# The four 64-column matmuls of each state-space group pair: alternating between PSUM's halves, and held together

## The chip, the cores and the metric

The kernel runs on one core of a Trainium2 chip. A core has a matrix engine (TensorE), engines for elementwise work (VectorE, ScalarE, GpSimd), queues that issue transfers (SyncE among them), an on-chip memory of 128 partitions (SBUF) and a smaller one for matmul results (PSUM, also 128 partitions, in eight banks). The metric is the time on the device in microseconds (us), taken as the median over runs. Lower is better.

## The reference

One layer of a hybrid encoder, in float32, for 2048 tokens of width 1024. A normalised input goes through one wide projection, which feeds three branches: a "forgetting" attention of 12 heads, a state-space layer with a gated unit, and a cross attention into 256 memory tokens. The gated branches are projected back, merged, projected once more and added to the input. The part that matters here is the state-space layer, 48 groups of 16 channels, each with 64 complex states:

```python
    x_re = jnp.einsum('gph,blgh->blgp', bb_re, uf)
    x_im = jnp.einsum('gph,blgh->blgp', bb_im, uf)
    ...
    _, _, h_re, h_im = lax.associative_scan(combine, (a_re, a_im, x_re, x_im), axis=1)
    y = (jnp.einsum('ghp,blgp->blgh', c_re.astype(f32), h_re)
         - jnp.einsum('ghp,blgp->blgh', c_im.astype(f32), h_im))
    y = y + d_skip.astype(f32).reshape(S5_GROUPS, S5_GROUP) * uf
```

The state runs over the tokens with a complex decay; the output is a linear function of the state plus a direct term.

## The kernel before

The large matrix products are made from float32 operands that are split into a high and a low part; `mm3` (lines 144 to 149) issues three matmuls for each product: high by high (line 147), the stationary operand's high by the moving one's low part (148), and the other way round (149). One projection chunk is an output tile of 128 channels by 512 tokens, 24 such matmuls into one PSUM bank (`proj_chunk`, tags `psA` and `psF`).

The state-space branch works in the shadow of these projections. `gen_s5` goes through 24 pairs of groups; `s5_pair` (from line 534) treats one pair, in chunks of 8 tokens:

- VectorE builds the matrix that says what a chunk adds to the state (`m1r`, `m1i`); TensorE transposes both (lines 550, 551), ScalarE copies them to SBUF (`m1t`).
- VectorE builds `z` and `bb`, from the decay's powers and the input and output matrices. Two matmuls of 16 output columns (line 572, tile `psB`) make the kernel by which a chunk's inputs act on its own outputs. ScalarE copies it (574), and nine transfers bring it through device memory into a banded matrix `m3`.
- Four matmuls of 64 output columns (line 585, tile `psC`) make what each chunk adds to the state: for each of the two groups, the real and the imaginary part. Their stationary operand is a slice of `m1t`, their moving one the pair's inputs `u` (256 columns). Group 0 writes PSUM partitions 0 to 63, group 1 partitions 64 to 127; real and imaginary part stand beside each other, so all four write one bank.
- VectorE builds a table of phases (lines 588 to 596), reads the four results (598 to 602), runs two real scans (605, 606) and turns the states back (`hs`).
- Four matmuls of 128 columns (625, 626) make the outputs from `m3`, `u`, `z` and `hs`; ScalarE copies them out, a transfer stores them.

```python
        pv = self.psC()
        for g in range(2):
            for ri in range(2):
                nc.tensor.matmul(pv[64 * g:64 * g + 64, ri * 256:(ri + 1) * 256],
                                 m1t[:, ri * 128 + 64 * g:ri * 128 + 64 * g + 64], u[:, g, :], start=True, stop=True)
```

Each step ends with a `yield`. `proj` alternates: for each projection chunk the side work may take some 1.7 steps (`RATE[0]`). This sets the program order, which is the order of priority. The order in which an engine gets its instructions is set by a planner: it simulates the kernel while it is built, and at each moment gives an engine the ready instruction that stands earliest in the program. An engine then works its queue off in that order. `issue_after(x)` tells the planner that what a block issues on the engine of `x` may be queued only behind `x`; it doesn't wait for the result of `x`. The kernel already uses it near its end (line 1038), to tie projection work to the attention.

Of the kernel before, what the change touches and what calls it, by code (L numbers as in the profile page):

```python
# [12 lines left out]
D = 1024  # L13
# [3 lines left out]
KD = 8  # L17
# [17 lines left out]
KS = 3  # L35
# [14 lines left out]
class Layer:  # L50
# [83 lines left out]
    def load_w(self, src, shape, pool=None, bufs=2):  # L134
        """One [128, 1024] slab of weights, split into two float32r parts."""
        raw = self.wp.tile([128, 4 * NV], F32, tag="wraw", name="wraw", bufs=2)
        k, m = shape
        n = k * m
        self.nc.sync.dma_start(out=raw[:, :n], in_=src)
        hi, lo = ((pool or self.wp).tile([128, n if bufs == 1 else 1024], F32R, tag=t, name=t, bufs=bufs) for t in ("whi", "wlo"))  # L140
        self.split(hi[:, :n], lo[:, :n], raw[:, :n])
        return (hi[:, :n].rearrange("p (k m) -> p k m", k=k), lo[:, :n].rearrange("p (k m) -> p k m", k=k))

    def mm3(self, out, a, b, first, last):
        """a = (hi, lo) stationary, b = (hi, lo) moving."""
        nc = self.nc
        nc.tensor.matmul(out, a[0], b[0], start=first, stop=False)  # L147
        nc.tensor.matmul(out, a[0], b[1], start=False, stop=False)  # L148
        nc.tensor.matmul(out, a[1], b[0], start=False, stop=last)  # L149

    def rsqrt(self, p, out, ssq, n):
        """out = 1 / sqrt(ssq / D + eps): table square root, then a Newton step."""
        nc = self.nc
        v = p.tile([128, n], F32, tag="nv", name="nv", bufs=2)
        t = p.tile([128, n], F32, tag="nt", name="nt", bufs=2)
        nc.vector.tensor_scalar(out=v, in0=ssq, scalar1=1.0 / D, scalar2=EPS, op0=ALU.mult, op1=ALU.add)
        nc.scalar.activation(t, v, AF.Sqrt)
        nc.vector.reciprocal(out, t)
        nc.vector.tensor_mul(t, out, out)
        nc.vector.tensor_mul(t, t, v)  # L160
        nc.vector.tensor_scalar(out=t, in0=t, scalar1=-0.5, scalar2=1.5, op0=ALU.mult, op1=ALU.add)
        nc.vector.tensor_mul(out, out, t)

    def norm_T(self, src, nt, g, hi, lo, p, xb, split=False):
        """RMSNorm of nt tiles of 128 tokens, then transposed and split: hi, lo [128, KD, nt*128]."""
        nc = self.nc
# [23 lines left out]

# [1 line left out]
    def open_h(self):  # L192
# [63 lines left out]
    def proj_v(self, g, p):  # L256
        """Values of four heads; the forget gates ride with the first four."""
        nc, s = self.nc, self.s
# [29 lines left out]
    def forget(self, p):  # L288
        """-F, the running sum of -log sigmoid(z)."""
        nc, z = self.nc, self.fz  # L290
        e = p.tile([H, L], F32, name="fe")
        nc.vector.scalar_tensor_tensor(out=e, in0=z, scalar=-1.0, in1=z, op0=ALU.mult, op1=ALU.max)
        nc.scalar.activation(e, e, AF.Exp, scale=-1.0)
        nc.scalar.activation(e, e, AF.Ln, bias=1.0)
        nc.vector.scalar_tensor_tensor(out=z, in0=z, scalar=0.0, in1=e, op0=ALU.min, op1=ALU.subtract)
        one = p.tile([H, 1], F32, name="fo")
        nc.vector.memset(one, 1.0)
        nc.vector.tensor_tensor_scan(e, one.to_broadcast([H, L]), z, 0.0, ALU.mult, ALU.subtract)
        nc.sync.dma_start(out=self.s["nf"], in_=e)
# [106 lines left out]

# [1 line left out]
    def s5_exp(self, p, out, x):  # L408
        """exp(x): range reduction by ln 2, polynomial, exact power of two."""
        v = self.nc.vector  # L410
# [14 lines left out]
    def s5_reduce(self, t, n):  # L425
        """t - 2 pi round(t / 2 pi), in place."""
        v = self.nc.vector
        v.tensor_scalar(out=n, in0=t, scalar1=0.15915494309189535, scalar2=12582912.0, op0=ALU.mult, op1=ALU.add)
        v.tensor_scalar(out=n, in0=n, scalar1=-12582912.0, scalar2=None, op0=ALU.add)
        for c in (6.28125, 2029.0 / 1048576.0, 3.0199159819e-7):  # L430
            v.scalar_tensor_tensor(out=t, in0=n, scalar=-c, in1=t, op0=ALU.mult, op1=ALU.add)

    def s5_sincos(self, p, sn, cs, t, n):
        """sin and cos of t in [-pi, pi] (t is overwritten) by the quarter angle and two doublings."""
        v = self.nc.vector
# [16 lines left out]
    def cmul(self, outr, outi, ar, ai, br, bi, t):  # L452
        """(outr, outi) = (ar, ai) (br, bi); t is scratch; the outputs are none of the inputs."""
        v = self.nc.vector
        v.tensor_mul(outr, ar, br)
        v.tensor_mul(t, ai, bi)
        v.tensor_sub(outr, outr, t)
        v.tensor_mul(outi, ar, bi)
        v.tensor_mul(t, ai, br)
        v.tensor_add(outi, outi, t)  # L460

    def s5_prep(self, q, p):
        """Discretised parameters in the layout [(group parity, state), group pair]; q keeps, p is scratch."""
        nc, v, i = self.nc, self.nc.vector, self.i
# [69 lines left out]
    def s5_pair(self, q, a):  # L534
        """Groups 2a and 2a+1. Chunks of 8 steps: what a chunk adds to the state (M1), the state at each chunk's
        end (a real scan of the states turned back by the phase they have run through), and the outputs from the
        state before the chunk (M2) and from the chunk's own inputs (M3)."""
        nc, v, s = self.nc, self.nc.vector, self.s
# [32 lines left out]
        for g in range(2):  # L571
            nc.tensor.matmul(ps[0:16, g * 128:(g + 1) * 128], bb[:, g, :], z[:, g, 0:128], start=True, stop=True)
        kd = q.tile([16, 2, 128], F32, tag="kd", name="kd", bufs=1)
# [8 lines left out]
        pv = self.psC()  # L582
        for g in range(2):
            for ri in range(2):
                nc.tensor.matmul(pv[64 * g:64 * g + 64, ri * 256:(ri + 1) * 256],  # L585
                                 m1t[:, ri * 128 + 64 * g:ri * 128 + 64 * g + 64], u[:, g, :], start=True, stop=True)
        er, ei, vr, vi, x, hr = t("er", 256), t("ei", 256), t("vr", 256), t("vi", 256), t("xx", 256), t("hr", 256)
# [53 lines left out]

# [1 line left out]
    def mem_scores(self, p, hd, j, b, P):  # L643
# [56 lines left out]

# [1 line left out]
    def open_fox(self):  # L702
# [3 lines left out]
    def fox_keys(self, h, c):  # L706
        """Half a head's keys (high over low parts), values (high beside low) and -F."""
        nc, s, p = self.nc, self.s, self.fp
# [21 lines left out]
    def fox_scores(self, p, hd, q, G, P):  # L730
        """Softmax rows of two blocks of 128 queries, the later one first: the mask goes into -F for good, as no
        later block of queries is left to read those keys unmasked."""
        nc = self.nc
# [31 lines left out]
    def fox_pv(self, p, h, hd, G, P):  # L765
        """Columns of the moving operand and of the sums: high parts of the two query blocks, then low parts."""
        nc, s = self.nc, self.s
# [41 lines left out]
    def gen_fox(self):  # L809
        """Heads one after the other, groups of queries from the last to the first; a head's last KS groups, the  # L810
        short ones, alternate with the next head's first ones."""
        p, self.close_f = self.pool("fox", side="right")
# [32 lines left out]

# [1 line left out]
    def gen_glu(self):  # L847
# [39 lines left out]
    def split(self, hi, lo, x, sc=1.0):  # L887
        """sc * x as hi + lo, each exact in float32r."""
        self.nc.gpsimd.tensor_scalar(out=hi, in0=x, scalar1=sc, scalar2=1.0, op0=ALU.mult, op1=ALU.mult)  # L889
# [7 lines left out]
    def ytile(self):  # L897
        """Slots of 4 KB, twelve in the first pool and ten in the second, in the order in which they come free."""
        i, self.ny = self.ny, self.ny + 1
# [20 lines left out]
    def gen_merge0(self):  # L920
        """The last chunk, under the last heads; its share of the attention as soon as the last head is past it."""
        nc, c = self.nc, NC - 1
# [129 lines left out]

# The channels of the state-space branch are kept, 128 at a time, in the order (channel of a group, group).
def host_arrays(x, mem, g_norm, g_mem_norm, g_final, w_in, b_forget, b_merge, w_mem_kv,
# [68 lines left out]
```

## Time and profile before

| | |
|---|---|
| time, median of 3 runs | 3076.02 us (3070.25 to 3080.53) |
| span of the profiled execution (its only time on the page) | 3072.7 us |
| TensorE matmuls, busy | 2995.7 us (97%) |
| VectorE, busy | 1884.8 us (61%) |
| GpSimd, busy | 1004.8 us (33%) |
| ScalarE, busy | 927.8 us (30%) |
| first and last start of the matmuls of line 585 | 405.3 and 927.1 us |
| granted TensorE clock, mean | 0.987 |

The profile is taken from one execution. "Busy" is the union of the times in which an engine has an instruction in flight; matmuls are pipelined, so several records can overlap, and the time from one start to the next says more than a duration. A float32 matmul of line 585 or 572 leaves two records. "L585" is line 585 of the kernel; `psC<-u,m1t` reads: writes `psC`, from `u` and `m1t`; "128*64" is the stationary operand (128 rows, 64 columns), "128x256" the moving one.

### The profile page before, as it was taken

The numbers are of one execution on the slowest core, as the hardware profiler recorded it, in microseconds if no ns is written. First come the engines' busy times: TensorE is split into PE (matmuls) and PEld (weight loads), VectorE is DVE, ScalarE is ACT, GpSimd is POOL, SyncE is SP. The second block draws the span as 40 slices with busy tenths as digits, with TensorE's granted clock in tenths as the row PEclk, the third lists the DMA queues.
The fourth block names the chain that finished last, engine by engine and source line by source line (L and its number), as shares of the span: only waits on it lengthen the run. The fifth ranks groups of instructions, "written<-read, shape, count | busy, mean of one in ns | idle before, by whom it ended". The sixth has DMA issues, their size and how long they took to land.

```text
span 3072.7 us, 43527 instructions
## 1 busy us (share of the span) xinstructions
PE 2995.7 (97%) x14656; PEld 2438.1 (79%) x14656; DVE 1884.8 (61%) x4982; ACT 927.8 (30%) x1881; POOL 1004.8 (33%) x1328
## 2 busy tenths in 40 slices
PE   9999999999999999999999999999999998999999
PEld 7889977777777778888878888888887786777787
DVE  5333489888886673322217777777777886555544
ACT  5102111111112231222216666666666550000011
POOL 0010000000001332121205665655555766555500
PEclk9999999999999999999999999999999998999999
DMA  5343323323344655344352443544434536665531
GB/s 167 107 136 96 105 84 116 115 84 111 114 132 150 175 164 173 108 127 136 115 165 82 124 121 103 134 121 121 118 111 130 145 108 195 185 182 172 159 108 69
DMA packets 283118, 396.81 MB, mean 129 GB/s; under 512 B 83060, under 2 KB 147828, under 8 KB 282884
## 3 DMA queue, kind: packets, MB, share of 16 engines
q1 hardware_dynamic: 275696, 381.39, 41.8%
q10 hardware_dynamic: 7200, 12.66, 1.2%
q8 instruction: 116, 1.90, 0.3%
q14 instruction: 106, 0.87, 0.1%
HBM read 265.51 MB, written 128.42 MB: 128 GB/s over the span
## 4 chain that ended last, share of the span: by engine, by line
PE 80%; DMA 6%; DVE 5%; issue 4%; POOL 3%; ACT 1%; SPq 0%; DVEq 0%; POOLq 0%; ACTq 0%
PE psF L147 10%; PE psF L148 10%; PE psF L149 10%; PE psA L147 8%; PE psA L148 8%; PE psA L149 8%; PE psC L798 5%; PE psB L782 5%; PE psA L750 3%; PE psA L751 3%; PE psC L147 1%; PE psC L148 1%; PE psC L149 1%; PE psC L585 1%; PE psB L149 1%
## 5 line engine op out<-in xcount | busy, mean ns | idle before, releaser
L147 PE MATMUL psF<-hh,whi 128*128 128x512 f32 (+1 forms) x1160 | 470.2, 405 | 5.3 <-DVE elo L228 2.5
L889 POOL TENSOR_SCALAR whi<-wraw 128x1024 fp32r<-128x1024 f32 (+2 forms) x216 | 204.8, 949 | 795.2 <-PE psA L148 362.0
L149 PE MATMUL psF<-hh,wlo 128*128 128x512 f32 (+1 forms) x1160 | 460.5, 397 | 0.5 <-DVE wlo L891 0.5
L148 PE MATMUL psF<-hl,whi 128*128 128x512 f32 (+1 forms) x1160 | 460.7, 397 | 0.0
L891 DVE TENSOR_TENSOR wlo<-wraw,whi 128x1024 fp32r<-128x1024 f32 (+2 forms) x216 | 260.5, 1207 | 213.4 <-POOL whi L889 189.2
L147 PE MATMUL psA<-hh,whi 128*128 128x512 f32 (+1 forms) x816 | 322.5, 397 | 1.4 <-ACT hh L187 0.8
L148 PE MATMUL psA<-hl,whi 128*128 128x512 f32 (+1 forms) x816 | 322.9, 396 | 0.0
L149 PE MATMUL psA<-hh,wlo 128*128 128x512 f32 (+1 forms) x816 | 321.7, 395 | 0.8 <-DVE wlo L891 0.8
L786 DVE TENSOR_TENSOR Pt<-psB,Pt 128x512 fp32r<-128x512 f32 x336 | 226.2, 685 | 76.3 <-ACT Pt L785 73.9
L798 PE MATMUL psC<-Pt,v 128*128 128x512 f32 x864 | 266.7, 398 | 4.1 <-DVE Pt L786 3.5
L147 PEld LDWEIGHTS psF<-hh,whi 128*128 128x128 f32 x1160 | 219.6, 189 | 52.7 <-DVE elo L228 3.3
L149 PEld LDWEIGHTS psF<-hh,wlo 128*128 128x128 f32 x1160 | 219.5, 189 | 52.0 <-DVE wlo L891 0.9
L148 PEld LDWEIGHTS psF<-hl,whi 128*128 128x128 f32 x1160 | 219.8, 189 | 45.8 <-issue 0.4
L752 DVE CUSTOM_DVE_ANT_0 P<-psA,nf 128x512 f32<-128x512 f32 (+1 forms) x336 | 201.2, 627 | 48.1 <-PE psA L751 28.2
L785 ACT CAST Pt<-psB 128x512 fp32r<-128x512 f32 x336 | 191.9, 586 | 107.4 <-PE psB L782 60.4
L761 POOL TENSOR_SCALAR P<-P,rd 128x768 f32<-128x768 f32 (+1 forms) x240 | 193.2, 821 | 59.6 <-DVE rd L758 36.6
L750 PE MATMUL psA<-kk,qh 128*128 128x512 f32 (+1 forms) x480 | 184.1, 389 | 4.5 <-DVE mx L752 2.6
L147 PEld LDWEIGHTS psA<-hh,whi 128*128 128x128 f32 x816 | 154.1, 189 | 36.9 <-issue 1.6
L149 PEld LDWEIGHTS psA<-hh,wlo 128*128 128x128 f32 x816 | 154.5, 189 | 36.1 <-DVE wlo L891 1.2
L148 PEld LDWEIGHTS psA<-hl,whi 128*128 128x128 f32 x816 | 154.3, 189 | 33.9 <-issue 0.4
L798 PEld LDWEIGHTS psC<-Pt,v 128*128 128x128 f32 x864 | 154.2, 190 | 31.2 <-DVE Pt L786 6.8
L782 PE MATMUL psB<-ident,P 128*128 128x128 f32 x1200 | 177.4, 274 | 0.3 <-POOL P L761 0.2
(343 smaller groups left out, 6228.3 us busy)
## 6 DMA issues: line engine op xcount, KB each, us to landing
wraw<-in_w_in SPq DMA_DIRECT2D x90, 512.0 KB, 4.3
s_gl<-ehi SPq DMA_DIRECT2D x96, 256.0 KB, 2.5
g<-s_gl SPq DMA_DIRECT2D x96, 256.0 KB, 4.6
wraw<-in_w_proj SPq DMA_DIRECT2D x64, 320.0 KB, 2.9
s_vs<-ev_v SPq DMA_DIRECT2D x48, 256.0 KB, 2.7
nf<-s_nf SPq DMA_DIRECT2D x24, 512.0 KB, 6.4
v<-s_vs SPq DMA_DIRECT2D x24, 512.0 KB, 6.4
qh<-s_qh SPq DMA_DIRECT2D x96, 128.0 KB, 3.7
```

Source lines behind the costliest of these rows:

```text
L147: nc.tensor.matmul(out, a[0], b[0], start=first, stop=False)
L148: nc.tensor.matmul(out, a[0], b[1], start=False, stop=False)
L149: nc.tensor.matmul(out, a[1], b[0], start=False, stop=last)
L750: nc.tensor.matmul(ps[:, :wm], q[0][:, qs], kk[:, c0:c0 + wm], start=True, stop=False)
L752: nc.vector.tensor_tensor_reduce(out=pr[:, c * 512:c * 512 + w], in0=ps[:, :w], in1=nf[:, c0:c0 + w], scale=1.0, scalar=-3.0e38, op0=ALU.a ...
L761: nc.gpsimd.tensor_scalar(out=c, in0=c, scalar1=rd, scalar2=0.5, op0=ALU.mult, op1=ALU.mult)
L782: nc.tensor.transpose(ps[:, o:o + 128], P[b][:, kt * 128:(kt + 1) * 128], self.ident)
L785: nc.scalar.copy(hi, psv)
L786: nc.vector.tensor_sub(lo, psv, fl32(hi))
L798: self.pe = nc.tensor.matmul(o, v, m, start=(kt == 0), stop=(kt == 2 * G + 1))
L889: self.nc.gpsimd.tensor_scalar(out=hi, in0=x, scalar1=sc, scalar2=1.0, op0=ALU.mult, op1=ALU.mult)
L891: self.nc.vector.tensor_sub(lo, x, fl32(hi))
```

## The change

The second chunk-kernel matmul is kept by name (`last`), and the four matmuls of line 585 are issued inside a block that puts them behind it. Inside the block the two loops change places: the outer one goes over real and imaginary part, the inner one over the groups, so that consecutive matmuls write different halves of PSUM's partitions. Operands, results and their number stay. The rest of the difference takes out comments and doc strings, in place, so line numbers move by one behind line 583 only.

```diff
         ps = self.psB()
         for g in range(2):
-            nc.tensor.matmul(ps[0:16, g * 128:(g + 1) * 128], bb[:, g, :], z[:, g, 0:128], start=True, stop=True)
+            last = nc.tensor.matmul(ps[0:16, g * 128:(g + 1) * 128], bb[:, g, :], z[:, g, 0:128], start=True, stop=True)
...
         pv = self.psC()
-        for g in range(2):
+        with self.tc.issue_after(last.ins):
             for ri in range(2):
-                nc.tensor.matmul(pv[64 * g:64 * g + 64, ri * 256:(ri + 1) * 256],
-                                 m1t[:, ri * 128 + 64 * g:ri * 128 + 64 * g + 64], u[:, g, :], start=True, stop=True)
+                for g in range(2):
+                    nc.tensor.matmul(pv[64 * g:64 * g + 64, ri * 256:(ri + 1) * 256],
+                                     m1t[:, ri * 128 + 64 * g:ri * 128 + 64 * g + 64], u[:, g, :], start=True, stop=True)
```

## The prediction

> **What bounds the kernel now.** I read the page first (busy time, then the costliest groups), then the busy time of every engine by stretches of the run, because the change touches one stretch only.
>
> ```profile
> span 3072.7 us, 43527 instructions
> PE 2995.7 (97%) x14656; PEld 2438.1 (79%) x14656; DVE 1884.8 (61%) x4982; ACT 927.8 (30%) x1881; POOL 1004.8 (33%) x1328
> ```
>
> ```profile
> core 0: us, PE busy (x) PEld busy (x) DVE busy (x) ACT busy (x) POOL busy (x), PEclk, DMA share, GB/s
> 400.00:945.00 545.00, 545.00 (x2411) 417.78 (x2410) 470.16 (x1701) 78.40 (x152) 24.47 (x43) 1.00 0.33 108
> 945.00:1200.00 255.00, 246.47 (x1031) 194.11 (x1030) 165.13 (x199) 70.60 (x96) 87.72 (x78) 0.99 0.57 165
> 1628.00:2540.00 912.00, 892.71 (x4781) 740.66 (x4780) 673.05 (x1999) 562.51 (x1140) 557.98 (x795) 0.99 0.43 119
> ```
>
> TensorE is busy 97% of the span, and in the stretch of the state-space branch (400 to 945 us) it is busy for all of the 545.00 us, at full clock (1.00). VectorE comes next there, with 470 of 545 us (86%). So time that TensorE doesn't need in this stretch is time saved, unless something else ends up late.
>
> Next, the changed matmuls by themselves (instructions by source line, and groups with shapes kept apart). The columns of a group are: line, engine, operation, operands, shapes, count, then busy us and mean ns of one.
>
> ```profile
> L585 PE MATMUL psC<-u,m1t x192: 379/379/431, 405.3 to 927.1; 128*64 128x256 f32 x192
> ```
>
> ```profile
> L585 PE MATMUL psC<-u,m1t 128*64 128x256 f32 x192 | 44.9, 393 | 0.0
> L572 PE MATMUL psB<-z,bb 128*16 128x128 f32 x96 | 14.7, 275 | 0.0
> ```
>
> The 24 group pairs give 192 records, so one of these float32 matmuls leaves two records, and a pair's four leave eight. I call these eight the pack. The two small matmuls that make the chunk kernel (line 572) leave four records a pair. A mean duration says little here, since records overlap. I therefore went to the order of time around each pack, TensorE only, and found three shapes. These three pairs have only projection matmuls (lines 147 to 149) on both sides. Columns: start us, us from first start to last end, engine, line, operation, count.
>
> ```profile
> 765.41 0.40 PE L149 MATMUL psF<-hh,wlo 128*128 128x512 f32 x1
> 765.74 1.08 PE L585 MATMUL psC<-u,m1t 128*64 128x256 f32 x4
> 766.75 0.61 PE L572 MATMUL psB<-z,bb 128*16 128x128 f32 x4
> 767.29 1.08 PE L585 MATMUL psC<-u,m1t 128*64 128x256 f32 x4
> 768.30 0.50 PE L147 MATMUL psF<-hh,whi 128*128 128x512 f32 x1
> ```
>
> ```profile
> 857.13 0.40 PE L148 MATMUL psA<-hl,whi 128*128 128x512 f32 x1
> 857.46 0.65 PE L585 MATMUL psC<-u,m1t 128*64 128x256 f32 x2
> 858.03 0.61 PE L572 MATMUL psB<-z,bb 128*16 128x128 f32 x4
> 858.57 1.08 PE L585 MATMUL psC<-u,m1t 128*64 128x256 f32 x6
> 859.59 0.50 PE L149 MATMUL psA<-hh,wlo 128*128 128x512 f32 x1
> ```
>
> ```profile
> 744.18 0.39 PE L149 MATMUL psA<-hh,wlo 128*128 128x512 f32 x1
> 744.42 0.40 PE L147 MATMUL psA<-hh,whi 128*128 128x512 f32 x1
> 744.74 0.61 PE L572 MATMUL psB<-z,bb 128*16 128x128 f32 x4
> 745.28 1.09 PE L585 MATMUL psC<-u,m1t 128*64 128x256 f32 x8
> 746.31 0.50 PE L148 MATMUL psA<-hl,whi 128*128 128x512 f32 x1
> ```
>
> In the first shape (split 4 + 4) the chunk-kernel matmuls stand in the middle of the pack, and four records fill 1.08 us on each side. In the third (whole) all eight records fill 1.09 us. So eight in a row take no longer than four: two streams run at once, and with 64 output columns each, these must be the two halves. In the second shape (2 + 6) six records after the interruption also fill 1.08 us; in the code's order they are the first group's second matmul, then both of the second group, so two neighbours of different halves overlap and the last runs alone.
>
> How often each shape occurs comes from the busy time of line 585 alone, one stretch per pair. Quoted are the first and last row of each shape; the values 2.15 to 2.16 occur 14 times, 1.73 six times, 1.09 four times.
>
> ```profile
> core 0: us, PE busy (x) PEld busy (x), PEclk, DMA share, GB/s
> 404.30:407.20 2.90, 1.09 (x8) 0.51 (x8) 1.00 0.69 187
> 424.60:428.60 4.00, 1.73 (x8) 0.66 (x8) 1.00 0.18 67
> 447.50:451.90 4.40, 2.15 (x8) 0.93 (x8) 1.00 0.00 0
> ...
> 744.30:747.20 2.90, 1.09 (x8) 0.50 (x8) 1.00 0.48 182
> ...
> 900.70:904.70 4.00, 1.73 (x8) 0.66 (x8) 1.00 0.35 130
> 923.90:928.30 4.40, 2.15 (x8) 0.93 (x8) 1.00 0.33 119
> sum 97.90, PE 44.91 PEld 19.02; mean PE 1.87 PEld 0.79
> ```
>
> **The change, part by part.** It adds and removes no instruction, no transfer and no buffer. It does two things to the four matmuls: their program order becomes group 0, 1, 0, 1, and all four may be issued only behind the second chunk-kernel matmul.
>
> What a pair costs the stream is the time from the projection matmul before to the one after, less the 0.23 us in which projection matmuls otherwise follow each other (744.42 − 744.18 = 0.24; longer runs of them give 0.23).
>
> Split 4 + 4: 768.30 − 765.41 − 0.23 = 2.66 us. Split 2 + 6: 859.59 − 857.13 − 0.23 = 2.23 us. Whole, behind the chunk kernel: 746.31 − 744.42 − 0.23 = 1.66 us.
>
> The held-back pack can't be split by the chunk kernel any more, so every pair should take the third shape. Gain: 14 × (2.66 − 1.66) + 6 × (2.23 − 1.66) + 4 × 0 = 14.0 + 3.4 = **17.4 us**. Line 585's busy time should fall by about 14 × 1.06 + 6 × 0.64 = 18.7 us, from 44.9 to about 26; that is more than the gain, because the records' tails overlap their neighbours.
>
> The new order within the pack I cost at nothing against the third shape. Its bounds: whether the planner kept the code's order there or not, eight adjacent records ran in two streams; the 2 + 6 row shows that neighbours of different halves overlap. The most the alternation can lose is all overlap, which is a rival below.
>
> The hold adds a wait in TensorE's own queue only. What is late if the chunk kernel is late? Behind it stand the pack, then VectorE's line 598, which reads the pack, and then the rest of VectorE's queue. The closest case I found is the pair at 516 us, where the chunk kernel's last input was written at 511.82 + 1.47 = 513.29 and its first matmul started at 516.80:
>
> ```profile
> 511.82 1.47 DVE L568 SCALAR_TENSOR_TENSOR z<-x,x 64x144 f32<-64x144 f32 x2
> ```
>
> ```profile
> 516.80 0.61 PE L572 MATMUL psB<-z,bb 128*16 128x128 f32 x4
> ```
>
> That leaves 3.5 us of slack, against a move forward of at most 1.01 us (the four records that no longer stand ahead, 765.74 to 766.75). The pack's end relative to the chunk kernel stays put: the last projection matmul follows 768.30 − 766.75 = 1.55 us after it in the first shape, 746.31 − 744.74 = 1.57 in the third. VectorE therefore waits no longer than before. The chunk kernel's copy on ScalarE and its nine transfers on SP's queue are issued behind it, as before, up to 1.0 us earlier in the stream; they move past nothing on those queues. If the slack were gone, each microsecond of lateness would cost 24 us over the pairs.
>
> What lies between the two bounds of the gain: if the planner set the pack apart from the chunk kernel, with projection matmuls in between, both would pay an entry and an exit of their own. The chunk kernel alone has a row:
>
> ```profile
> 402.00 0.40 PE L149 MATMUL psA<-hh,wlo 128*128 128x512 f32 x1
> 402.32 0.61 PE L572 MATMUL psB<-z,bb 128*16 128x128 f32 x4
> 402.87 0.50 PE L147 MATMUL psA<-hh,whi 128*128 128x512 f32 x1
> ```
>
> It costs 402.87 − 402.00 − 0.23 = 0.64 us. A whole pack alone costs the 1.03 us of 745.28 to 746.31, plus the 0.32 us of an entry, less 0.23, so 1.12. Together that is 1.76 instead of 1.66, so the gain would be 17.4 − 24 × 0.10 = 15.0 us. I take 17.4, since in all three quoted shapes the planner put the chunk kernel and the pack together. Upwards I see 0.2 us (the first pair, whose pack stands alone now).
>
> The sum is made against the profiled span, 3072.7 us; the page has no other time of that execution. The timed runs go from 3070.25 to 3080.53 with a median of 3076.02, 3.3 us above the span and within their spread. I take the 3.3 us as unchanged: 3076.0 − 17.4 = **3058.6 us**, −0.57%.
>
> **The rivals.** *Adjacent, but one after another.* If alternating halves lost the overlap, eight records would follow at the pace of one half. That pace is (1.08 − 0.65) / 2 = 0.215 us from the rows with four and two records. The pack would take 768.30 − 767.29 + 4 × 0.215 = 1.87 us instead of 1.03, and the pair 2.50 instead of 1.66. The sum: 14 × (2.50 − 2.66) + 6 × (2.50 − 2.23) + 4 × (2.50 − 1.66) = +2.7 us, so 3078.7, no change. Against it stand the rows with 8 records in 1.09 us and with 6 in 1.08. The Trainium skill, "TensorE: Matmul & The Clock Gate", section "Part 3: Packing small matmuls — row/col tiling", would speak for this rival: it says that a weight load overlaps a matmul in flight only when its row group differs, and both halves here use all 128 rows. The trace of this case disagrees, since two halves' matmuls with their loads fit into the time of one.
>
> *The planner gives it back.* All instruction orders come from a planner that simulates the whole kernel; a different order in 24 places can shift what it does later. What can be lost is idle time of TensorE: it is 0 in the stretch itself, 255.00 − 246.47 = 8.5 us in the next and 912.00 − 892.71 = 19.3 us in the attention stretch. If it grew there by as much as the gain, the time would be 3076. For it: those stretches have waits of several us. Against it: nothing in them has a fixed time, so they can move ahead as a whole.
>
> *Slower: the pack falls apart.* The hold lets all four go at the same moment, but projection matmuls that stand earlier in the program may be ready too. If the planner deals the four out singly among them, each pays an entry and an exit and has no partner. The 2 + 6 shape prices one: 858.03 − 857.13 − 0.23 = 0.67 us. A pair would cost 0.64 + 4 × 0.67 = 3.32 us. Now a pair costs (14 × 2.66 + 6 × 2.23 + 4 × 1.66) / 24 = 2.39 on the mean. All pairs single gives +24 × 0.93 = 22 us, 3098 us. It decides from (2.39 − 1.66) / (3.32 − 1.66) = 44% of the pairs on. Against it: in none of the 24 packs of the trace does a projection matmul stand between records of line 585, although they were the planner's to place.
>
> **How the numbers follow.** Forecast 0.75 (3053 to 3064, with the spread of the timed runs); pack apart from the chunk kernel 0.05 (3061); one after another 0.04 (3079); given back, wholly or by more than half, 0.10 (3067 to 3078); falls apart 0.06 (up to 3098). A measurement of this kernel tells about 0.3% from no change, which is 9.2 us; so faster means below 3066.8. Forecast and pack apart are faster, nearly always: 0.79. Same: 0.04 + 0.10 = 0.14, with a little from the edges. Slower: 0.07. Range 3050 to 3070: the forecast with its spread, the pack apart, and the nearer part of what could be given back; the upper end leaves out the other rivals.
>
> **What would show it.** In the profile after: line 585 busy for about 26 us instead of 44.9, 1.09 us in each of the 24 pairs; eight records in one row behind four of the chunk kernel; the end of the last pack near 910 us instead of 927; TensorE without idle time in the stretch; chunk-kernel copies and line 598 not waiting longer than now. Wrong would be: eight records in 1.9 us (no overlap), projection matmuls between records of a pack, idle TensorE ahead of the chunk kernel, or a pack end 17 us earlier with later stretches longer by as much.

## The result and the profile after

The changed kernel takes 3054.21 us (median of 4 runs, 3053.40 to 3061.56) against 3075.83 us before. The ratio is 0.994, with a 95% interval of 0.992 to 0.996. The forecast was 3058.6 us with a range of 3050 to 3070. Two later comparisons (below) gave ratios of 0.9952 and 0.9950, so the gain is about half a per cent.

The page of the changed kernel, its span and busy times:

```profile
span 3059.8 us, 43529 instructions
PE 2973.6 (97%) x14656; PEld 2425.4 (79%) x14656; DVE 1885.2 (62%) x4982; ACT 927.3 (30%) x1881; POOL 1005.5 (33%) x1328
```

The profiled execution was the slowest of the four (its time was 3061.56). So the two spans differ by 12.9 us only, while TensorE's busy time fell by 2995.7 − 2973.6 = 22.1 us. Neither number alone is the gain; the stages show why.

The pack in the changed kernel, first its instructions by source line (shortest, median and longest in ns, first and last start), then in order of time for a pair that has projection matmuls on both sides:

```profile
L586 PE MATMUL psC<-u,m1t x192: 379/379/430, 405.0 to 913.4; 128*64 128x256 f32 x192
```

```profile
780.04 0.40 PE L148 MATMUL psF<-hl,whi 128*128 128x512 f32 x1
780.37 0.61 PE L572 MATMUL psB<-z,bb 128*16 128x128 f32 x4
780.91 1.08 PE L586 MATMUL psC<-u,m1t 128*64 128x256 f32 x8
781.93 0.50 PE L149 MATMUL psF<-hh,wlo 128*128 128x512 f32 x1
```

The pair costs 781.93 − 780.04 − 0.23 = 1.66 us, the number used in the forecast. Line 586 (585 before) is busy for 26.0 us instead of 44.9, the sum in the next rows: its busy time by pair, one stretch each, first and last of 24 that all show 1.08:

```profile
404.00:406.90 2.90, 1.08 (x8) 0.48 (x8) 1.00 0.65 203
...
911.70:914.60 2.90, 1.08 (x8) 0.48 (x8) 1.00 0.49 181
sum 69.60, PE 26.02 PEld 11.63; mean PE 1.08 PEld 0.48
```

Next, all engines by stages, cut at the same events in both kernels: first pack, last matmul of the state-space branch, last of the gated unit, first and last of the attention's value products, end. Columns: stretch, its length, then the busy time of each engine with its count. Before:

```profile
core 0: us, PE busy (x) PEld busy (x) DVE busy (x) ACT busy (x) POOL busy (x), PEclk, DMA share, GB/s
405.30:941.40 536.10, 536.10 (x2371) 411.23 (x2371) 465.46 (x1688) 75.39 (x146) 23.39 (x42) 1.00 0.34 109
941.40:1194.60 253.20, 244.67 (x1023) 192.66 (x1023) 163.42 (x197) 71.09 (x97) 86.67 (x77) 0.99 0.57 165
1194.60:1628.00 433.40, 430.18 (x2007) 352.36 (x2005) 121.75 (x262) 104.78 (x235) 83.11 (x170) 1.00 0.45 134
1628.00:2536.20 908.20, 890.76 (x4773) 739.40 (x4773) 672.52 (x1998) 562.14 (x1139) 557.23 (x795) 0.99 0.43 119
2536.20:3072.70 536.50, 499.38 (x2037) 391.96 (x2036) 293.06 (x415) 28.34 (x83) 227.29 (x216) 0.96 0.49 153
```

And after:

```profile
405.00:927.40 522.40, 522.40 (x2388) 407.22 (x2388) 465.20 (x1689) 76.15 (x147) 23.24 (x42) 1.00 0.35 113
927.40:1178.50 251.10, 240.68 (x1006) 189.94 (x1006) 160.50 (x196) 70.32 (x96) 89.83 (x77) 0.98 0.57 165
1178.50:1612.80 434.30, 430.19 (x2007) 352.36 (x2005) 121.72 (x262) 104.74 (x235) 83.08 (x170) 1.00 0.45 133
1612.80:2521.20 908.40, 889.52 (x4774) 737.22 (x4774) 672.66 (x1998) 561.69 (x1139) 557.27 (x795) 0.99 0.42 119
2521.20:3059.80 538.60, 497.62 (x2037) 389.01 (x2035) 296.93 (x415) 28.35 (x83) 224.48 (x216) 0.97 0.49 152
```

The state-space stretch is 13.7 us shorter, and TensorE has no idle time in it, before and after. It also holds 2388 − 2371 = 17 more matmuls, and the gated unit's stage 17 fewer: the planner moved projection matmuls forward. Over the first three rows TensorE is busy for 1210.95 us before and 522.40 + 240.68 + 430.19 = 1193.27 after. The difference is **17.7 us**, and the sum of the forecast was 17.4. Of these, 15.2 us have arrived when the attention starts (1612.8 instead of 1628.0). The rest is in idle time of TensorE, which is a stage's length less its busy time: the gated unit's stage has 10.4 us of it instead of 8.5, the stage behind it 4.1 instead of 3.2. The last two stages differ by a few us, which is no more than they spread within one program (below).

### The profile page after: what moved, and what is told of

It is laid out like the page before. It is cut to its first block, busy times and chain, and to the rows that moved or that the text cites. A ratio compares the mean times of both kernels' runs of the same rounds, so it can differ in the third digit from the quotient of the medians.

```text
span 3059.8 us, 43529 instructions
## 1 busy us (share of the span) xinstructions
PE 2973.6 (97%) x14656; PEld 2425.4 (79%) x14656; DVE 1885.2 (62%) x4982; ACT 927.3 (30%) x1881; POOL 1005.5 (33%) x1328
## 4 chain that ended last, share of the span: by engine, by line
PE 80%; DMA 7%; DVE 5%; POOL 3%; issue 3%; ACT 1%; SPq 0%; DVEq 0%; POOLq 0%; ACTq 0%
PE psF L147 10%; PE psF L148 10%; PE psF L149 10%; PE psA L149 8%; PE psA L147 8%; PE psA L148 8%; PE psC L799 5%; PE psB L783 5%; PE psA L751 3%; PE psA L752 3%; PE psC L147 2%; PE psC L149 2%; PE psC L148 2%; PE psB L149 1%; PE psB L147 1%
```

## The experiments

**Size of the gain, and what spreads.** The changed kernel was timed twice more, and the kernel before was profiled once more.

> The changed kernel once more, to size the gain over more runs. Theory A (adjacency: matmuls of the two halves overlap whenever both halves have one waiting at TensorE's head, and TensorE time saved in this stretch is kernel time one for one): 17.4 us less than before, by the record's sum. Rival C (the first comparison's 21.6 us is real, so something beyond the pack got faster, or part is given back): clearly more than 20 or less than 14 us. Line 586 busy 24 x 1.09 = about 26 us in both.

> The changed kernel once more, beside the run that follows, on one chip. By the traces so far 14 to 18 us less than the kernel before.

> The kernel before once more, for a second trace of the same instruction order: each stage's length again. If the stages after the state-space branch repeat within 1 us, differences there between kernels come from the order; if they spread by several us, such differences say nothing. Expected: the state-space stretch repeats within 1 us (405 to 927.5 us), the attention and output stages spread by 3 to 5 us.

Measured: 3053.75 us against 3070.16 before (ratio 0.9952, 0.9940 to 0.9963), and 3054.90 against 3068.95 (0.9950, 0.9936 to 0.9964). That is 16.4 and 14.1 us; with the first comparison's 21.6 they lie around the 17.4 of the sum. The changed kernel's three medians (3054.21, 3053.75, 3054.90) agree; the kernel before had 3075.83 in the first runs and is at 3069 to 3070 in these. So the first 21.6 owes what it has over the other two to its reference. The second trace of the kernel before, same stages:

```profile
405.90:942.10 536.20, 536.20 (x2372) 411.62 (x2372) 465.51 (x1688) 75.28 (x146) 23.31 (x42) 1.00 0.33 109
942.10:1197.20 255.10, 244.51 (x1023) 192.72 (x1022) 163.99 (x197) 71.09 (x97) 86.64 (x77) 0.99 0.57 164
1197.20:1631.50 434.30, 430.24 (x2008) 352.53 (x2006) 121.81 (x262) 104.73 (x235) 82.81 (x170) 1.00 0.44 133
1631.50:2537.50 906.00, 888.50 (x4774) 738.65 (x4774) 675.05 (x1998) 561.83 (x1139) 556.10 (x795) 0.99 0.42 119
2537.50:3071.20 533.70, 495.73 (x2037) 387.80 (x2035) 292.41 (x415) 28.35 (x83) 226.38 (x216) 0.97 0.48 153
```

and of the changed kernel:

```profile
404.70:927.20 522.50, 522.50 (x2389) 407.81 (x2389) 465.13 (x1689) 76.07 (x147) 23.15 (x42) 1.00 0.35 112
927.20:1178.40 251.20, 241.77 (x1006) 190.75 (x1005) 160.62 (x196) 70.28 (x96) 89.37 (x77) 0.98 0.56 165
1178.40:1612.80 434.40, 429.98 (x2007) 352.69 (x2005) 121.75 (x262) 104.73 (x235) 82.77 (x170) 1.00 0.44 133
1612.80:2516.70 903.90, 888.33 (x4774) 738.39 (x4774) 672.78 (x1998) 561.96 (x1139) 556.28 (x795) 0.99 0.42 120
2516.70:3052.00 535.30, 498.33 (x2037) 391.27 (x2035) 293.61 (x415) 28.35 (x83) 225.93 (x216) 0.96 0.48 153
```

The state-space stretch repeats to 0.1 us in each kernel (536.1 and 536.2; 522.4 and 522.5). The attention and the output stage spread by 2 to 5 us within one and the same program (908.2 and 906.0, 908.4 and 903.9; 536.5 and 533.7, 538.6 and 535.3). The start of the attention spreads too (1628.0 and 1631.5 before, 1612.8 twice after). What repeats best, beside the stretch, is TensorE's busy time over the first three rows: 1210.95 us in both traces before, 1193.27 and 1194.25 after. By this measure the change is worth 16.7 to 17.7 us.

**The hold without the alternation.** The four stay in the order group 0, 0, 1, 1, held behind the chunk kernel.

```diff
         with self.tc.issue_after(last.ins):
-            for ri in range(2):
-                for g in range(2):
+            for g in range(2):
+                for ri in range(2):
```

> The four matmuls are held behind the chunk kernel, but stay in the order group 0, 0, 1, 1. Theory A: the halves overlap all the same, since the whole packs of the kernel before ran eight records in 1.09 us; the same time as the changed kernel within 3 us. Rival B (order: matmuls go to the array strictly in their order, so that two of the same half in front block the other half): a pack takes 1.87 us instead of 1.03, a pair 2.50, and the kernel is at about 3079, some 20 to 25 us over the changed one.

Measured: 3056.24 us (ratio to before 0.9957, 0.9945 to 0.9969), beside 3053.75 for the changed kernel: not to be told apart. The pack, in order of time:

```profile
781.05 0.40 PE L148 MATMUL psF<-hl,whi 128*128 128x512 f32 x1
781.37 0.61 PE L572 MATMUL psB<-z,bb 128*16 128x128 f32 x4
781.91 1.09 PE L586 MATMUL psC<-u,m1t 128*64 128x256 f32 x8
782.93 0.50 PE L149 MATMUL psF<-hh,wlo 128*128 128x512 f32 x1
```

Eight records again fill 1.09 us, here and in the other 23 pairs (26.18 us in all), and the pair costs 782.93 − 781.05 − 0.23 = 1.65. The state-space stretch takes 522.6 us with 2389 matmuls, beside 522.5 with as many in the changed kernel's second trace. In the built program's instruction list the order is 0, 0, 1, 1 in every pair, and the trace shows that it is another order than the changed kernel's: the pack's second record starts 13 to 15 ns behind the first in every pair, against 6 to 8 ns there. If matmuls started strictly in that order, group 1 could begin with group 0's fourth record at the earliest, 3 × 0.215 = 0.65 us in, and its own four records would take the 1.08 us that four of one half took before: 1.73 us for the pack, not 1.09. The rival of order falls: with the hold in place the alternation does nothing. The Trainium skill, "TensorE: Matmul & The Clock Gate", section "Part 3: Packing small matmuls — row/col tiling", says that matmuls start in program order, without reordering; the 1.09 us here disagree, for matmuls of different halves.

**The alternation without the hold.**

```diff
-        with self.tc.issue_after(last.ins):
-            for ri in range(2):
-                for g in range(2):
+        for ri in range(2):
+            for g in range(2):
```

> The four matmuls alternate between the halves, but nothing holds them behind the chunk kernel, so the planner may again split the pack by it. Theory A: a pack split 2 + 2 still has both halves on each side and costs 2.66 - 2 x 0.43 = 1.8 us, one split 1 + 3 or 3 + 1 costs about 2.23, a whole one 1.66 to 1.76; with some 13 packs split 1 + 3 or 3 + 1, six 2 + 2 and five whole that is 13 x 2.23 + 6 x 1.8 + 5 x 1.7 = 48 us, against 57 before and 40 in the changed kernel: about 9 us faster than before and 9 slower than the changed one. Rival B: the alternation is what counts, so nearly all of the gain is here, the time within 4 us of the changed kernel's.

Measured: 3058.42 us (ratio 0.9961, 0.9947 to 0.9975), 11.7 us faster than before and 4.7 slower than the changed kernel of the same runs; the two intervals overlap. The 4.7 us lie between what the two theories expected (9, and under 4), so time alone doesn't decide between them; the trace does. Line 585 by pair: 1.08 or 1.09 five times, 1.30 or 1.31 six times, 1.72 or 1.73 thirteen times; the first row of each value, and a late one of the two split ones:

```profile
403.60:406.50 2.90, 1.08 (x8) 0.49 (x8) 1.00 0.70 195
423.90:427.90 4.00, 1.72 (x8) 0.66 (x8) 1.00 0.18 66
446.80:450.40 3.60, 1.31 (x8) 0.40 (x8) 1.00 0.01 2
...
753.40:757.00 3.60, 1.30 (x8) 0.40 (x8) 1.00 0.39 146
...
914.70:918.70 4.00, 1.73 (x8) 0.66 (x8) 1.00 0.37 135
```

A pack split two and two, in order of time:

```profile
667.21 0.40 PE L147 MATMUL psF<-hh,whi 128*128 128x512 f32 x1
667.53 0.65 PE L585 MATMUL psC<-u,m1t 128*64 128x256 f32 x4
668.12 0.61 PE L572 MATMUL psB<-z,bb 128*16 128x128 f32 x4
668.65 0.65 PE L585 MATMUL psC<-u,m1t 128*64 128x256 f32 x4
669.24 0.50 PE L148 MATMUL psF<-hl,whi 128*128 128x512 f32 x1
```

It costs 669.24 − 667.21 − 0.23 = 1.80 us, where the kernel before paid 2.66 for the same split with one half on each side. The chunk kernel still splits 19 of 24 packs, and 13 of them leave one matmul without a partner (1.72). The state-space stretch of this trace:

```profile
404.60:931.50 526.90, 526.90 (x2367) 405.17 (x2367) 465.20 (x1688) 75.41 (x146) 23.64 (x42) 1.00 0.34 111
```

It is 536.10 − 526.90 = 9.2 us shorter than before and holds 2371 − 2367 = 4 projection matmuls fewer, worth 4 × 0.23 = 0.9 us, so 8.3 us come from the packs: close to the 9 of theory A. Reckoned in the same way, the changed kernel has 13.7 + 17 × 0.23 = 17.6 us. Theory B falls. What the measured 11.7 us have over 8.3 isn't in the changed stretch, and is no more than the later stages spread. So each part of the change does something alone: the alternation makes a split cheaper, the hold makes splits impossible, and with the hold the alternation has nothing left to do.

**Is TensorE time in this stretch kernel time?** The pack is issued twice in a row.

```diff
-            for ri in range(2):
+            for ri in (0, 1, 0, 1):
```

> The changed kernel with the pack issued twice in a row (the second writes the same values again), which adds eight records in two streams to each pair. Theory A: 4 x 0.215 = 0.86 us a pair of pure TensorE time, 24 x 0.86 = 20.6 us more than the changed kernel, one for one. Rival C: if other waits of the stretch took up TensorE time, clearly less, under 12 us. If the halves didn't overlap it would be 24 x 1.72 = 41 us.

Measured: 3076.36 us, 22.6 more than the changed kernel in the same runs. The doubled pack in order of time:

```profile
427.10 1.95 PE L586 MATMUL psC<-u,m1t 128*64 128x256 f32 x16
```

Sixteen records take 1.95 us against 1.08 for eight, so 0.87 us a pair and 20.9 us in all. The kernel lost all of it, within the uncertainty: the state-space stretch is 20.3 us longer (542.7 instead of 522.4), and TensorE is busy for all of it. This also answers whether the halves overlap in a longer row: they do, at the pace of 0.215 us for two records.

**The same for the chunk kernel.** Its two matmuls of 16 columns write the same partitions. The first of two kernels puts group 1 into the other half (and copies the result out in two pieces); the second also pads the stationary operand with zeros to 64 columns, so that the chunk kernel and the pack have one shape. The second:

```diff
-            last = nc.tensor.matmul(ps[0:16, g * 128:(g + 1) * 128], bb[:, g, :], z[:, g, 0:128], start=True, stop=True)
+            last = nc.tensor.matmul(ps[64 * g:64 * g + 64, 0:128], bb[:, g, :], z[:, g, 0:128], start=True, stop=True)
...
-        nc.scalar.copy(kd, ps[0:16, 0:256].rearrange("p (g n) -> p g n", g=2))
+        for g in range(2):
+            nc.scalar.copy(kd[:, g, :], ps[64 * g:64 * g + 16, 0:128])
```

(`bb` is then one tile of 2 x 64 columns for all pairs, set to zero once; in the first kernel it stays as it was and the output is `ps[64 * g:64 * g + 16, 0:128]`.)

> The changed kernel, and the two chunk-kernel matmuls (16 columns) get the same treatment: group 1 writes partitions 64 to 79 instead of 0 to 15 of the next columns, so that the two lie in different halves; ScalarE copies them out in two pieces instead of one. Theory A (different halves overlap when adjacent): their four records, now 109 ns apart, run two by two, which saves 2 x 0.109 = 0.22 us a pair, 5.2 us in all: 3048 to 3050 where the changed kernel has 3054. Against it: the order of the planner shifts, which moved the gated-unit stage by up to 5 us between the kernels so far; and 24 more copies on ScalarE (0.3 us each), which is busy for 84 of 545 us in the stretch.

> As the run before, but the chunk kernel's stationary operand is padded with zeros to 64 columns, so that it and the pack are of one shape (64 columns). If the 0.20 us between the last chunk-kernel record and the first of the pack, against 0.11 between neighbours, is the price of changing the shape, this saves another 0.09 us a pair, 2.2 us in all: 3046 to 3048. If that gap has another cause (a wait, the longer moving operand), the time is that of the run before.

> The kernel with the padded chunk kernel in two halves, beside the changed kernel on one chip. Its trace shows 0.32 us a pair less for chunk kernel and pack (1.33 instead of 1.65 us), 7.7 us in all: 6 to 8 us less than the changed kernel if TensorE time counts one for one, 21 to 25 us less than the kernel before.

Measured: 3050.53 us (ratio to before 0.9941, 0.9928 to 0.9955) for the first; 3046.72 (0.9933, 0.9920 to 0.9945) and, beside the changed kernel's 3054.90 on one chip, 3044.27 (0.9916, 0.9901 to 0.9931) for the second. A pair of the first kernel, then of the second:

```profile
913.55 0.39 PE L149 MATMUL psA<-hh,wlo 128*128 128x512 f32 x1
913.87 0.40 PE L572 MATMUL psB<-z,bb 128*16 128x128 f32 x4
914.20 1.08 PE L587 MATMUL psC<-u,m1t 128*64 128x256 f32 x8
915.21 0.50 PE L147 MATMUL psA<-hh,whi 128*128 128x512 f32 x1
```

```profile
902.36 0.40 PE L149 MATMUL psF<-hh,wlo 128*128 128x512 f32 x1
902.69 0.44 PE L574 MATMUL psB<-z,bb 128*64 128x128 f32 x4
902.96 1.03 PE L589 MATMUL psC<-u,m1t 128*64 128x256 f32 x8
903.92 0.50 PE L147 MATMUL psF<-hh,whi 128*128 128x512 f32 x1
```

The pair costs 915.21 − 913.55 − 0.23 = 1.43 us in the first (1.66 − 0.22 = 1.44 expected) and 903.92 − 902.36 − 0.23 = 1.33 in the second (1.44 − 0.09 = 1.35 expected). The second is faster than the changed kernel by 10.6 us on the same chip, with intervals that don't overlap. That is more than the 6 to 8 that were expected; the rows account for 24 × 0.33 = 7.9 of it. In both of its traces the state-space stretch takes 514.5 us with 2388 matmuls, 7.9 less than the changed kernel's 522.4 with as many, so the other 2.7 us aren't from this stretch. It is the fastest version of this study. The padding alone, 1.43 against 1.33 us a pair, shows in the rows only: the times of the two kernels (3050.53 and 3046.72) have intervals that overlap. A price for changing the shape would explain the 0.10 us, but the two kernels differ in the operand's width too, so it isn't shown by itself. The Trainium skill, "TensorEngine Tiling (Array Packing)", section "Tiling Modes", says that a change of the tiling mode empties the array; the 0.10 us agree with that.

## Why the prediction was right

*TensorE bounds the stretch, one for one.* Right: TensorE has no idle time in the stretch in any trace shown, and 20.9 us of added TensorE time cost 22.6.

*Three shapes, and the third for every pair.* Right to 0.01 us: 24 rows of 1.08, a sum of 26.0, a pair of 1.66. The first pair's pack still stands apart from its chunk kernel, as before, so the 0.2 us that were foreseen for it didn't come.

*Gain of 17.4 us.* Right: TensorE's busy time to the start of the attention fell by 16.7 to 17.7; three timed comparisons gave 21.6, 16.4 and 14.1. The forecast of 3058.6 took the median of the first three runs of the kernel before as its base, some 6 us above the same kernel's later medians; that, and not the gain, is why it lies 4.4 us over the measured 3054.21.

*Order within the pack costs nothing.* Right, and stronger than said: once the pack is whole, 0, 0, 1, 1 and 0, 1, 0, 1 take the same time.

*The hold makes nothing late.* Right. What VectorE's reader of the pack waited for, before and after (idle us of the engine just before it, and times):

```profile
  PE psC L585: 12.3, 15
```

```profile
  PE psC L586: 0.6, 1
```

It waits less, not longer. Why is not shown. The gain doesn't hang on it: the padded chunk kernel gained another 7.9 us in the stretch while this wait stayed where it was (0.5 us, after 0.6).

*The end of the last pack near 910 us.* Off: the last record starts at 913.4. The term that was missing is the 17 projection matmuls that moved into the stretch, 17 × 0.23 = 3.9 us: 927.1 − 17.4 + 3.9 = 913.6. The forecast had taken the neighbours' order as fixed. For the total this changes nothing, since the next stage has them no more.

*The rivals.* "One after another" fell with the first trace (1.08 us). "The planner gives it back" isn't seen beyond the spread: the gated unit's stage idles 10.4 and 9.4 us in the two traces after, against 8.5 and 10.6 before, the attention 18.9 and 15.6 against 17.4 and 17.5. "Pack apart from the chunk kernel" is what the first pair does, in both kernels; the other 23 stand together. "Falls apart" didn't occur; a kernel with the pack dealt out singly among projection matmuls wasn't tried, so its price of 0.67 us for one is only argued.

## What to carry to other kernels

The matmuls of 64 output columns in this kernel, and those of 16, came two for the time of one when those of the two halves stood next to each other in TensorE's queue. So look in the order of time for small matmuls that a planner or a loop has separated, and cost the separation by the time from neighbour to neighbour, not by a mean duration. Keep a pack whole first (by an edge of order, for instance); its inner order is second. When later stages spread by about as much as the change is worth, measure the changed stage itself: its length, corrected for work that moved in or out, and the busy time of the engine that bounds it.

## What was not expected of the hardware

Matmuls of one half did not block those of the other half behind them: with the order 0, 0, 1, 1 the eight records took 1.09 us, the same as with 0, 1, 0, 1 (1.08). So TensorE didn't work its queue off strictly in order here. And the overlap holds for weight loads too, although both halves use all 128 rows: in the changed kernel eight loads of line 586 fit, with their matmuls, into 1.08 us a pair. In the pair at 780 us, the first two loads start 7 ns apart, and each takes 133 ns.
